# Neighbourhood stage: a third of the V loads and the gate-product stores on POOL's queue, bias tables asked for one unit sooner

## Chip, cores and metric

One core of a Trainium2 chip runs the whole kernel. The metric is device time in microseconds of one execution; the number given is the median of several runs. Engines are named as in the profile: PE (matmul), PEld (its weight loads), DVE (vector), ACT (scalar), POOL (GpSimd) and SP (which only issues transfers). "SPq" and "POOLq" are the transfers that SP and POOL issue.

## What is computed

One encoder layer on 1024 tokens (a 16 x 64 grid) with 1024 features: RMS norm, one input projection into eight parts, a dense differential attention (4 heads), a neighbourhood attention (8 heads), a gate on each, one output projection, a residual add, and a gated per-layer embedding. The part that the change touches:

```python
def neighbourhood_attention(q, k, v, rpb):
    # each query attends to its clamped 8 x 16 neighbourhood on the grid
    s = jnp.einsum('bhrcd,bhrikd->bhrcik', qg, kg) * (d ** -0.5) + bias[None]
    s = jnp.where(valid[:, None, :], s, NEG)
    pr = jax.nn.softmax(s.reshape(B, H, R, GRID_W, kr * GRID_W), axis=-1)
    o = jnp.einsum('bhrcik,bhrikd->bhrcd', pr, vg)
...
    ya = oa.transpose(0, 2, 1, 3).reshape(B, S, W_A) * jax.nn.silu(za)
    yb = neighbourhood_attention(qb, kb, vb, na_rpb[i]) * jax.nn.silu(zb)
```

## The kernel before

The program runs in stages: the input projection (to about 300 us), the neighbourhood attention (about 300 to 480), the differential attention (to about 670), and the output with the last gate. The order of the instructions on every engine is that of the Python code; there is no scheduler.

The neighbourhood stage works through 32 units: four pairs of heads (`pr`), two halves of the grid rows (`R`), four column strips (`j`). Unit 8 is the first of pair 1, unit 16 of pair 2, unit 24 of pair 3. A unit passes through these steps: `na_s` (PE: scores, line 647), `na_e` (DVE adds the bias table `Rt[pr]` and takes the minimum, line 662; ACT takes the exponential, line 667), `na_n` (DVE, lines 673 and 675), `na_t` (PE transposes, line 685; ACT copies out, line 687), `na_pv` (PE: times V, line 700) and `na_y` (DVE multiplies with the gate product into `nay`, line 710; ACT and POOL split it into a high and a low part `yb`, lines 715 and 716). After the eighth unit of a pair POOL stores both parts of `yb` to DRAM.

The stage's loop (line 1285) runs over i. Iteration i holds, in this order, `pre(i + 1)` (loads), `na_t` of unit i-1, `na_e` of unit i, `na_y` of unit i-2, `na_n` of unit i, `na_s` of unit i+1 and `na_pv` of unit i-1. Between them `fill` puts matmuls of the gate projection on PE (`z_mm`, lines 582 to 584), some ten matmuls per unit; each half of 512 tokens ends with ACT's tanh into `zth` (line 588) and DVE's product with the projection (`fin`, line 591). The product of a `zb` column stays in SBUF for `na_y`; that of a `za` column is stored to the DRAM tensor `uad` for the stage after, in two halves per column, eight stores in all.

`pre` (line 832) issues the loads: Q per half, K per pair, the two bias tables R of the next pair (`load_r`, 376 KB each), and with every unit the V window of the unit two further on (`load_v`, line 629): three transfers of 48 or 64 KB, each of four grid rows by 24 or 32 columns by 128 features. All loads go by `ld` on SP, one in-order queue; `stp` issues on POOL, another. The helper lines in the profile are 97 (`ld`), 100 (`st`) and 103 (`stp`).

SBUF tiles come from pools of rotating buffers. V windows, `nay` and `zth` share one pool of 11 buffers (tag `b2`), so a tile of the gate product frees its buffer for one of these only when its store has landed. R tables and the score tiles `nas` share one of 6.

Of the kernel before, what the change touches and what calls it, by code (L numbers as in the profile page):

```python
# [15 lines left out]
P = 128  # L16
# [8 lines left out]
COL = dict(qa=0, ka=512, va=1024, za=1536, qb=2048, kb=2560, vb=3072, zb=3584)  # L25
COL0 = (0, 8, 24, 40)
# [5 lines left out]
def ap_of(t, off, dims):  # L32
    return bass.AP(tensor=t.tensor, offset=t.offset + off, ap=[list(d) for d in dims])
# [7 lines left out]
def layer_kernel(ctx, tc, x, p, ngr, w_in, w_out, gains, lamv, t5p, rpbp, w_gate, w_ple,  # L41
# [22 lines left out]
    def T2(shape, dt=F32, n="t2"):  # L64
        return sb.tile(shape, dt, name=nm(n), tag="b2", bufs=NB2)

    def T15(shape, dt=F32, n="t15"):
        return sb.tile(shape, dt, name=nm(n), tag="b2", bufs=NB2)
# [14 lines left out]
    def PS(shape, n="ps"):  # L83
        return psp.tile(shape, F32, name=nm(n), tag="ps", bufs=4)
# [4 lines left out]
    def DT(shape, dt=F32, n="d"):  # L89
        n = nm(n)  # L90
        return dr.tile(shape, dt, name=n, tag=n, bufs=1)

    def raw(a):
        return a.bitcast(F32) if a.dtype == F32R else a

    def ld(o, i):
        return nc.sync.dma_start(raw(o), raw(i))  # L97

    def st(o, i):
        return nc.sync.dma_start(raw(o), raw(i))  # L100

    def stp(o, i):
        return nc.gpsimd.dma_start(raw(o), raw(i))
# [233 lines left out]
    def xh(kc, a, b):  # L337
        return xq(kc, a // 512)[0][:, kc % 4, a % 512:a % 512 + b - a]

    def xl(kc, a, b):  # L340
        return xq(kc, a // 512)[1][:, kc % 4, a % 512:a % 512 + b - a]
# [77 lines left out]
    vbd = DT([S, 512], n="vb")  # L419
# [147 lines left out]
    def z_low():  # L567
        while zl:
            zl.pop(0)()
# [5 lines left out]
    def z_mm(col, us):  # L575
        z_low()
        w = zw[col]
        for hf in range(2):
            a, b = hf * 512, hf * 512 + 512
            ps = PS([P, 512], "zps")  # L580
            for kc in range(8):
                mm(ps, w[:, 0, kc], xh(kc, a, b), start=(kc == 0), stop=False)  # L582
                mm(ps, w[:, 0, kc], xl(kc, a, b), start=False, stop=False)  # L583
                mm(ps, w[:, 1, kc], xh(kc, a, b), start=False, stop=(kc == 7))  # L584
                if kc < 7:
                    yield 3
            th = T2([P, 512], n="zth")
            act(th, ps, AF.Tanh, scale=0.5)

            def fin(th=th, ps=ps, hf=hf):  # L590
                V.scalar_tensor_tensor(th, th, 1.0, ps, op0=OP.add, op1=OP.mult)
                us[hf] = th
                if col < COL["qb"]:
                    st(uad[(col - COL["za"]) // P][:, hf * 512:hf * 512 + 512], th)

            zp.append(fin)
            yield 3


    uad = DT([4, P, S], n="uad")  # L600
# [6 lines left out]
    def load_k(pr):  # L607
        k1 = T8([P, 2, S], F32R, n="K1")
        h, l = qkd["kb"]
        for (dst, s) in ((k1[0:64], h), (k1[64:128], l), (K2[pr % 2][0:64], h)):  # L610
            ld(dst, s[pr].rearrange("(h d) s -> d h s", h=2))
        kb[pr] = k1

    def load_q(pr, R):
        q1 = T4([P, 2, 512], F32R, n="Q1")
        h, l = qkd["qb"]
        for (dst, s) in ((q1[0:64], h), (q1[64:128], h), (Q2[R][0:64], l)):
            ld(dst, s[pr, :, R * 512:(R + 1) * 512].rearrange("(h d) s -> d h s", h=2))
        qb[pr, R] = q1

    def load_r(pr):
        r = []
        for h in range(2):
            t = TA([P, 752], n="R")
            ld(t, ap_of(rpbp, (2 * pr + h) * 23 * 48 + 1, [[48, 8], [1, 16], [1, 752]]))
            r.append(t)
        Rt[pr] = r

    def load_v(pr, R, j):
        w = WID[j]  # L630
        v = T15([P, 3, P], n="Vw")
        for m in range(3):
            r0 = 4 * R + 4 * m
            ld(v[0:4 * w, m], ap_of(vbd, (r0 * 64 + COL0[j]) * 512 + pr * P, [[64 * 512, 4], [512, w], [1, P]]))
        Vw[pr, R, j] = v

    na = {}
# [194 lines left out]
    def pre(i):  # L832
        if i >= len(units):
            return
        pr, R, j = units[i]
        if j == 0:
            if R == 0:
                load_q(pr, 1)
            elif pr + 1 < 4:
                load_q(pr + 1, 0)  # L840
        if (R, j) == (0, 2) and pr + 1 < 4:
            load_k(pr + 1)
        if (R, j) == (1, 2) and pr + 1 < 4:
            load_r(pr + 1)
        if i + 2 < len(units):
            load_v(*units[i + 2])
# [89 lines left out]
    def s7():  # L936
# [14 lines left out]
        NS - 5: lambda: (load_r0(), x_reload()),  # L951
        NS - 4: lambda: (z_load(COL["zb"], True), z_load(COL["zb"] + P, True)),
        NS - 2: lambda: (na_consts_q(), load_q(0, 0), load_v(0, 0, 0), load_v(0, 0, 1), z_split(COL["zb"], 0, 4),
                         z_split(COL["zb"], 4, 8), z_low()),
        NS - 1: lambda: (pre(0), x_resplit()),
        NS: na_consts_k,
    }
# [327 lines left out]
    for i in range(NU + 3):  # L1285
        if i < NU:
            pre(i + 1)
# [171 lines left out]
```

## Time and profile before

| what | value |
|---|---|
| median of 3 runs | 829.63 us (827.16 to 831.23) |
| the execution profiled | 825.45 us |
| its span, first to last instruction | 823.7 us |
| PE busy | 781.7 us, 95% of the span |
| DVE, ACT, POOL busy | 514.6, 437.2 and 261.3 us |
| mean granted TensorE clock | 0.984 |
| SP's queue (q1) | 116688 packets, 145.39 MB |
| POOL's queue (q0) | 1792 packets, 5.77 MB |

The span is 1.75 us shorter than the execution. Busy time of PE counts matmuls, which are pipelined, so full stretches and holes are read from windows of time rather than from the share of the whole span. A row of the timeline gives the start and length of an instruction (or of neighbours merged into one row), its engine, its line, what it writes and reads, and in brackets the engine's idle time before it with what ended it.

### The profile page before, as it was taken

How to read it: one execution, taken by the hardware profiler on the slowest of the kernel's cores; microseconds unless marked ns; L12 is line 12 of the kernel's file. 1: busy time of each engine (PE TensorE's matmuls, PEld its weight loads, DVE VectorE, ACT ScalarE, POOL GpSimd, SP SyncE). 2: the span in 40 equal slices, each digit the busy share in tenths (PEclk: the TensorE clock that was granted, in tenths of full speed). 3: DMA queues.
4: the chain of work that ended last, by engine and by line, in shares of the span. 5: the costliest groups of instructions: out<-in, count | busy, mean ns of one | idle time of the engine just before them, and what ended most of it. 6: DMA issues, size and time to landing. Idle time of an engine off the chain costs nothing.

```text
span 823.7 us, 12188 instructions
## 1 busy us (share of the span) xinstructions
PE 781.7 (95%) x4242; PEld 647.9 (79%) x4242; DVE 514.6 (62%) x990; ACT 437.2 (53%) x814; POOL 261.3 (32%) x263
## 2 busy tenths in 40 slices
PE   7999899999989999797989988999999999999997
PEld 6788688888878887576867867888888877888886
DVE  4658976786997675445536568777777743732332
ACT  5765545254444545335635578888888852311120
POOL 1001433352655400011101035777777752100000
PEclk9999999999999999999989999999999999999999
DMA  8855363862889997585767578667577427122222
GB/s 318 321 199 185 120 212 101 283 156 85 237 262 239 239 307 198 142 232 164 213 174 194 168 219 231 169 173 209 162 211 192 161 96 281 77 89 91 93 87 90
DMA packets 118541, 151.94 MB, mean 184 GB/s; under 512 B 23848, under 2 KB 76744, under 8 KB 118352
## 3 DMA queue, kind: packets, MB, share of 16 engines
q1 hardware_dynamic: 116688, 145.39, 58.9%
q0 software_dynamic: 1792, 5.77, 2.1%
q8 instruction: 34, 0.56, 0.3%
q14 instruction: 27, 0.22, 0.1%
HBM read 104.96 MB, written 46.17 MB: 183 GB/s over the span
## 4 chain that ended last, share of the span: by engine, by line
PE 65%; DMA 11%; DVE 11%; ACT 5%; issue 3%; SPq 3%; POOL 2%; DVEq 0%; ACTq 0%; POOLq 0%
PE dsp L1066 6%; PE ips L234 6%; PE ips L236 6%; PE ips L235 6%; PE gps L1261 4%; PE gps L1259 4%; PE gps L1260 4%; DMA Vw<-vb 3%; PE dtp L1108 3%; SPq L97 2%; PE ntp L685 2%; DMA wraw<-in_w_in_dram 2%; PE dpv L1135 2%; PE zps L582 2%; PE zps L584 2%
## 5 line engine op out<-in xcount | busy, mean ns | idle before, releaser
L234 PE MATMUL ips<-w,xh 128*128 128x512 f32 x336 | 134.0, 399 | 3.6 <-DVE C L260 3.0
L236 PE MATMUL ips<-w,xl 128*128 128x512 f32 x336 | 131.8, 392 | 0.0
L235 PE MATMUL ips<-w,xh 128*128 128x512 f32 x336 | 131.3, 391 | 0.0
L1091 POOL TENSOR_TENSOR s<-s,s 128x1024 f32<-128x1024 f32 x32 | 77.1, 2408 | 57.0 <-ACT s L1090 55.3
L433 POOL TENSOR_TENSOR qrs<-qms,nhalf 128x16 f32<-128x16 f32 x16 | 51.4, 3214 | 91.1 <-DVE qms L431 91.1
L1076 DVE CUSTOM_DVE_ANT_0 s<-dsp,T 128x1024 f32<-128x1024 f32 x64 | 77.7, 1215 | 2.5 <-PE dsp L1066 2.5
L234 PEld LDWEIGHTS ips<-w,xh 128*128 128x128 f32 x336 | 63.4, 189 | 17.1 <-issue 3.8
L1078 ACT ACTIVATE s<-s,dm 128x1024 f32<-128x1024 f32 x64 | 73.3, 1146 | 4.6 <-DVE dm L1076 4.5
L1066 PE MATMUL dsp<-K,Q 128*128 128x512 f32 x256 | 69.7, 394 | 4.9 <-DVE dm L1076 4.3
L236 PEld LDWEIGHTS ips<-w,xl 128*128 128x128 f32 x336 | 63.4, 189 | 13.8
L1115 DVE TENSOR_TENSOR aTl<-dtp,aTh 128x512 fp32r<-128x512 f32 x64 | 44.2, 691 | 48.0 <-ACT aTh L1109 48.0
L235 PEld LDWEIGHTS ips<-w,xh 128*128 128x128 f32 x336 | 63.6, 189 | 12.7
L716 POOL TENSOR_TENSOR yb<-nay,yb 128x128 fp32r<-128x128 f32 x32 | 16.4, 514 | 168.8 <-ACT yb L715 168.8
L218 DVE TENSOR_TENSOR w<-wraw,w 128x512 fp32r<-128x512 f32 x84 | 62.2, 778 | 5.6 <-ACT w L217 5.5
L687 ACT ACTIVATE PT<-ntp 96x768 f32<-96x768 f32 (+1 forms) x32 | 25.9, 810 | 63.0 <-PE ntp L685 63.0
L1066 PEld LDWEIGHTS dsp<-K,Q 128*128 128x128 f32 x256 | 45.9, 189 | 14.6 <-issue 3.1
L582 PE MATMUL zps<-xh,zw 128*128 128x512 f32 x128 | 54.2, 423 | 0.0
L584 PE MATMUL zps<-xh,zw 128*128 128x512 f32 x128 | 51.3, 401 | 0.0
L583 PE MATMUL zps<-xl,zw 128*128 128x512 f32 x128 | 51.1, 399 | 0.0
L217 ACT ACTIVATE w<-wraw 128x512 fp32r<-128x512 f32 x84 | 48.4, 626 | 4.7 <-DVE wraw L193 4.7
L1109 ACT ACTIVATE aTh<-dtp 128x512 fp32r<-128x512 f32 x64 | 38.0, 593 | 23.8 <-PE dtp L1108 23.7
L1259 PE MATMUL gps<-wgh,x1h 128*128 128x512 f32 x128 | 50.5, 395 | 0.0
(177 smaller groups left out, 1820.9 us busy)
## 6 DMA issues: line engine op xcount, KB each, us to landing
wraw<-in_w_in_dram SPq DMA_DIRECT2D x72, 256.0 KB
x<-in_x_dram SPq DMA_DIRECT2D x8, 512.0 KB
ppd<-pp SPq DMA_DIRECT2D x8, 512.0 KB
K<-kbh SPq DMA_DIRECT2D x8, 512.0 KB
Q<-qbh SPq DMA_DIRECT2D x16, 256.0 KB
Q<-qah SPq DMA_DIRECT2D x16, 256.0 KB
Q<-qal SPq DMA_DIRECT2D x16, 256.0 KB
wor<-in_w_out_dram SPq DMA_DIRECT2D x8, 512.0 KB
```

Source lines behind the costliest of these rows:

```text
L218: V.tensor_tensor(w[:, 1], r, w.bitcast(F32)[:, 0], op=OP.subtract)
L234: mm(ps, lh[:, k, a:a + P], w[:, 0], start=(new and k == 0), stop=False, skip_group_check=cont)
L235: mm(ps, lh[:, k, a:a + P], w[:, 1], start=False, stop=False, skip_group_check=cont)
L236: mm(ps, ll[:, k, a:a + P], w[:, 0], start=False, stop=(k == 3), skip_group_check=cont)
L433: G.tensor_tensor(rs, ms, nhalf, op=OP.pow)
L582: mm(ps, w[:, 0, kc], xh(kc, a, b), start=(kc == 0), stop=False)
L584: mm(ps, w[:, 1, kc], xh(kc, a, b), start=False, stop=(kc == 7))
L1066: mm(ps[:, cs], q[g][:, m, u * P:(u + 1) * P], k[:, cs], start=(g == 0), stop=(g == 1))
L1076: V.tensor_tensor_reduce(out=s, in0=ps, in1=back(Td[h][:, :], 1919 - (896 - P * qt), [[-1, S]]), scale=-1.0, scalar=BIG, op0=OP.add, op1=O ...
L1078: act(s, s, AF.Exp, bias=mx, scale=-1.0, accum_out=z[:, m:m + 1])
L1091: G.tensor_tensor(s1, s1, s2, op=OP.add)
L1259: mm(ps, h[:, k], wh, start=(k == 0), stop=False)
```

## The change

Three edits. The store of a `za` gate product goes by `stp` instead of `st`, so POOL issues it. Of the three transfers of a V window the third goes by `stp`, so POOL issues that too; the first two stay on SP. The bias tables of the next pair are asked for with unit (1, 1) instead of (1, 2), which is one unit sooner in the loop.

```diff
@@ z_mm, fin
                 if col < COL["qb"]:
-                    st(uad[(col - COL["za"]) // P][:, hf * 512:hf * 512 + 512], th)
+                    stp(uad[(col - COL["za"]) // P][:, hf * 512:hf * 512 + 512], th)
@@ load_v
         for m in range(3):
             r0 = 4 * R + 4 * m
-            ld(v[0:4 * w, m], ap_of(vbd, (r0 * 64 + COL0[j]) * 512 + pr * P, [[64 * 512, 4], [512, w], [1, P]]))
+            (ld if m < 2 else stp)(v[0:4 * w, m], ap_of(vbd, (r0 * 64 + COL0[j]) * 512 + pr * P, [[64 * 512, 4], [512, w], [1, P]]))
@@ pre
-        if (R, j) == (1, 2) and pr + 1 < 4:
+        if (R, j) == (1, 1) and pr + 1 < 4:
             load_r(pr + 1)
```

On SP, at the first load of bias tables (for pair 1). `Vw` is a V window, `R` a bias table, `vb` and `in_rpb_dram` are their sources; the number tells tiles apart, x3 counts transfers:

```order
-L97 DMA Vw_2989<-vb_111 128x1x128 x3
-L97 DMA Vw_3041<-vb_111 96x1x128 x3
-L97 DMA R_3095<-in_rpb_dram 128x1x752
-L97 DMA R_3097<-in_rpb_dram 128x1x752
-L97 DMA Vw_3099<-vb_111 96x1x128 x3
-L97 DMA Vw_3151<-vb_111 128x1x128 x3
+L97 DMA Vw_2989<-vb_111 128x1x128 x2
+L97 DMA R_3041<-in_rpb_dram 128x1x752
+L97 DMA R_3043<-in_rpb_dram 128x1x752
+L97 DMA Vw_3045<-vb_111 96x1x128 x2
+L97 DMA Vw_3099<-vb_111 96x1x128 x2
+L97 DMA Vw_3151<-vb_111 128x1x128 x2
```

The tables stand one V window earlier, and every window has two transfers on SP instead of three. (A new tile name gets a new number, so Vw_3045 is the Vw_3041 of before.)

On POOL, around the first store of a gate product (at the end of pair 0; rows without a sign stood there before):

```order
+L103 DMA Vw_3316<-vb_111 96x1x128
+L103 DMA uad_115<-zth_3342 128x512
 L716 TENSOR_TENSOR yb_2963<-nay_3348,yb_2963 128x8x16
 L103 DMA ybh_116<-yb_2963 128x1024
 L103 DMA ybl_117<-yb_2963 128x1024
+L103 DMA Vw_3378<-vb_111 128x1x128
 L716 TENSOR_TENSOR yb_3403<-nay_3401,yb_3403 128x8x16
+L103 DMA Vw_3433<-vb_111 128x1x128
```

The third of a V window now stands ahead of each subtraction, and the store between a V third and a subtraction. The same place on SP loses the store:

```order
-L97 DMA Vw_3316<-vb_111 96x1x128 x3
-L100 DMA uad_115<-zth_3342 128x512
-L97 DMA Vw_3378<-vb_111 128x1x128 x3
+L97 DMA Vw_3316<-vb_111 96x1x128 x2
+L97 DMA Vw_3378<-vb_111 128x1x128 x2
```

On SP nothing waits for the gate product any more; the next V window follows the one before it.

## Rows read from the trace of the kernel before

**Rows 1.** Stretches: busy us (instructions) of PE, PEld, DVE, ACT, POOL; clock; DMA share; GB/s.

```profile
300.00:340.00 40.00, 37.97 (x243) 30.17 (x242) 24.84 (x75) 21.04 (x54) 2.98 (x6) 1.00 0.76 200
340.00:450.00 110.00, 96.01 (x636) 75.90 (x636) 52.84 (x174) 50.33 (x132) 13.53 (x25) 0.94 0.66 188
450.00:480.00 30.00, 30.00 (x199) 23.87 (x199) 15.96 (x46) 16.53 (x42) 3.07 (x7) 1.00 0.51 138
```

**Rows 2.** Timeline of PE, 340 to 430 us: start, length, engine, line, [idle before it].

```profile
348.69 1.65 PE L647 MATMUL nsp<-K,Q 128*128 128x384 f32 x4 [4.35 <-DVE nam L662]
...
373.14 0.88 PE L700 MATMUL npv<-PT,Vw 96*64 96x128 f32 x12 [1.50 <-ACT PT L687]
375.16 0.83 PE L685 MATMUL ntp<-idn,nas 128*96 128x128 f32 x6 [1.14 <-DVE nas L675]
...
385.64 1.02 PE L685 MATMUL ntp<-idn,nas 128*128 128x128 f32 x6 [1.84 <-DVE nas L675]
...
422.26 1.51 PE L685 MATMUL ntp<-idn,nas 128*128 128x128 f32 x6 [4.08 <-DVE nas L675]
```

**Rows 3.** Stretches behind the two long holes, same columns as rows 1.

```profile
348.70:353.25 4.55, 4.55 (x20) 3.47 (x21) 2.20 (x8) 0.80 (x3) 0.46 (x1) 0.50 0.83 192
422.30:428.40 6.10, 6.10 (x19) 4.88 (x19) 3.50 (x13) 2.20 (x6) 0.62 (x2) 0.50 0.74 226
```

**Rows 4.** Waits, 295 to 480 us: engine and line <- awaited: total us, times, longest.

```profile
DVE nas L662 <- DMA R<-in_rpb_dram: 7.6, 2, 6.0
...
ACT zth L588 <- DMA uad<-zth: 5.7, 1, 5.7
...
DVE nay L710 <- DMA uad<-zth: 5.1, 2, 4.1
```

**Rows 5.** Timeline of SP's queue: start and length of the issue.

```profile
339.58 1.29 SPq L97 DMA_DIRECT2D R<-in_rpb_dram  x2
...
363.84 1.22 SPq L100 DMA_DIRECT2D uad<-zth  x1
...
380.60 1.39 SPq L97 DMA_DIRECT2D R<-in_rpb_dram  x2
...
414.74 1.73 SPq L100 DMA_DIRECT2D uad<-zth  x1
...
418.90 1.35 SPq L97 DMA_DIRECT2D R<-in_rpb_dram  x2
```

**Rows 6.** Chain of work that ended last: start, length, what (transposes of unit 4).

```profile
326.66 0.79 PE ntp L685 x6
```

**Rows 7.** Timelines of DVE and ACT (the row L588).

```profile
348.17 0.46 DVE L662 CUSTOM_DVE_ANT_1 nas<-nsp,R 128x288 f32<-128x288 f32 x1 [1.51 <-DMA R<-in_rpb_dram]
...
356.60 0.69 DVE L591 SCALAR_TENSOR_TENSOR zth<-zth,zps 128x512 f32<-128x512 f32 x1 [5.17 <-ACT zth L588]
...
371.80 0.60 ACT L588 ACTIVATE zth<-zps 128x512 f32<-128x512 f32 x1 [5.74 <-DMA uad<-zth]
...
389.94 0.45 DVE L662 CUSTOM_DVE_ANT_1 nas<-nsp,R 128x288 f32<-128x288 f32 x1
...
405.49 0.68 DVE L591 SCALAR_TENSOR_TENSOR zth<-zth,zps 128x512 f32<-128x512 f32 x1
...
421.30 0.29 DVE L710 TENSOR_TENSOR nay<-npv,zth 128x128 f32<-128x128 f32 x1 [4.11 <-DMA uad<-zth]
...
433.13 0.45 DVE L662 CUSTOM_DVE_ANT_1 nas<-nsp,R 128x288 f32<-128x288 f32 x1
```

**Rows 8.** POOL: issues of line 103 (ns min/median/max), their landing, and subtractions (busy, mean ns).

```profile
L103 POOL DMA_DIRECT2D ybh<-yb x4: 571/580/721, 358.3 to 480.1; - x4
...
DMA to landing us min/median/max: 4.3/7.0/10.4
...
L716 POOL TENSOR_TENSOR yb<-nay,yb 128x128 fp32r<-128x128 f32 x32 | 16.4, 514 | 168.8 <-ACT yb L715 168.8
```

**Rows 9.** Stretch around the first R issue, same columns as rows 1.

```profile
338.00:341.00 3.00, 2.03 (x10) 1.64 (x10) 1.11 (x3) 1.18 (x5) 0.46 (x1) 1.00 0.32 84
```

## Prediction

> **What bounds the kernel now.** I read the sums by stretch first. In the neighbourhood stage (about 300 to 480 us) PE, the matmul engine, is the busiest: 30.00 of 30 us in the last stretch, 37.97 of 40 in the first, but 96.01 of 110 in the middle, with a granted clock of 0.94 there and 1.00 on either side [rows 1]. So the stage is bound by PE, except for 14.0 us of holes and a slower clock between 340 and 450. Next PE in order of time: five holes make 12.9 of these 14.0 us, 4.35 before unit 9's scores at 348.69, 1.50 and 1.14 near 374, 1.84 at 385.64 and 4.08 at 422.26 [rows 2]. [...]
>
> Then the waits, for who made the holes. DVE waited 7.6 us for the bias tables R, ACT 5.7 us once and DVE 5.1 us twice for stores of the gate product to `uad` [rows 4]. Both are transfers of SP's queue. SP reaches the first R load at 339.58 [rows 5], though the loop asks for it in iteration 5, whose first PE work, `na_t` of unit 4, starts at 326.66 [rows 6]: the queue runs 13 us behind the program. R is used at once when it lands, the second head at 348.17 [rows 7], 8.6 us after the issue. The stores are the same story: DVE ends the product at 357.29 (356.60 + 0.69), SP issues its store at 363.84, and ACT, whose next `zth` takes the stored tile's buffer, has idled 5.74 us when it goes on at 371.80; the third product ends at 406.17 (405.49 + 0.68), its store goes out at 414.74, and DVE's `nay` waits 4.11 us for it, to 421.30 [rows 5, 7]. The hole of 1.84 us is the second store, the remaining 1.0 of DVE's 5.1 us [rows 2, 4]. So three late stores and one late table make all five holes.
>
> **The change, part by part.**
>
> 1. *R one unit sooner.* R is put ahead of one unit's V loads, and of the seven units' loads ahead of it one third each is gone: ten issues fewer on SP before it (three for the unit passed, seven thirds). From one R pair to the next SP took 41.0 us (339.58 to 380.60 [rows 5]) for 39 issues (2 R, 24 V, 6 Q, 3 K, 2 gate weights, 2 stores), 1.05 us each. At that price R leaves SP 10.5 us sooner, at 329; at the price of an issue alone (1.29 us for the two R [rows 5], 0.65 each) 6.5 us sooner, at 333. PE lost 4.35 us by R, so either covers it: 4.35 + 2.28 = **6.6 us** gone.
>
> 2. *Stores from POOL's queue.* A store on POOL stands behind a V third and in front of a `yb` subtraction, and waits for the same DVE product. Nothing of SP's backlog stands ahead of it. POOL's own 512 KB stores land 4.3 to 10.4 us after issue, 7.0 in the median, and an issue takes 0.57 to 0.72 us of POOL [rows 8]. From the end of the product to the need there are 8.8 us for the first (357.29 to 366.06, where ACT's idle time began) and 11.0 us for the third (406.17 to 417.19) [rows 7]. The stores have half those bytes. So they are in time except at the slow end: 1.50 + 1.14 + 1.84 + 4.08 of holes and 3.05 of half clock, **11.6 us**.
>
> 3. *A third of the V loads from POOL.* 32 issues leave SP and come to POOL. No V load from POOL's queue is in this trace; the nearest rows are the 512 KB stores, 0.57 to 0.72 us an issue [rows 8]. POOL now has 0.51 us of work per unit [rows 8], and a unit takes 4.5 us (43.2 us from unit 16's first R use to unit 24's, less 7.1 us of hole and half clock, over eight [rows 7]). With 0.72 for the load it is 1.2 of 4.5: hidden beside PE. Without that cover it would be 32 x 0.72 = 23 us at the most, so the cover matters, and it is wide: 3.3 us a unit. The load is asked for about four units before `na_pv` reads it, 18 us against 10.4 at most for landing. What is queued behind it on POOL is a `yb` subtraction, whose reader is the store at the end of eight units. In the stage after, one store stands between POOL's additions, some 0.7 us once beside PE work.
>
> Sum: 18.2 us gone. What is late next? Between 340 and 450 the other 1.1 us of holes stay. The first stretch had 2.03 us of small holes in 40 us without any of these waits, the last none in 30 [rows 1]; at the first's rate 110 us would hold 5.6, so 4.5 may come back, at the last's none. The stretch resembles the first more (K, Q and R are still loaded), so I give back 2.5. Net 15.7 us: 825.45 - 15.7 = 809.8 for the execution profiled. That one lies 4.18 us under the median of the runs; the median becomes 829.63 - 15.7 = **813.9**, given as 814.
>
> A row that bears on steps 1 and 3: from 338 to 341 us, just around R's issue, the DMA engines moved 84 GB/s at a mean busy share of 0.32 [rows 9]. The six transfers directly ahead of R are V thirds, so a V third seems to keep few engines busy while the queue behind it stands. [...]
>
> **The rivals.**
>
> *The DMA engines stay the limit (chance 0.20).* If a V third from POOL occupies the same engines as one from SP, the seven thirds save R nothing; it gains only its place, three issues, 3.2 us, and the queue's pace stays. For: the share of 0.32 above, a few engines working while the rest wait. Then PE can't get far ahead of the tables. With 8.6 us from issue, the third pair (418.90 [rows 5]) is usable at 427.5 against a use at 433.13 [rows 7], 5.6 us of room, and 3.2 more for its place: PE comes forward 8.8 us at most until there, the rest is waited again. Time 829.63 - 8.8 = 820.8. [...]
>
> *The stores stay late (0.13).* POOL takes its list in order, and the V third ahead of the store waits for a buffer that PE or POOL itself frees. If that holds the store back as long as SP did (6.55 us for the first), the 11.6 us stay and only R's 6.6 go, less the 2.5: 825.5, on the edge of no change. Against: the buffer's last reader is an iteration old by then.
>
> *POOL becomes the bound: slower (0.07).* If an issue of 128 short rows takes POOL far longer than of 128 long ones, POOL's list per unit, 0.51 us and one issue, outgrows a unit's 4.5 us; `nay` buffers come free late and `na_y` and the V loads wait for them. It decides from 4.0 us an issue on, and at 4.6 it has eaten the gain (28 units at 0.56). At 5.0 us: 28.0 - 15.7 = 12.3 us slower, 842. Against: 0.57 to 0.72 in the nearest rows.
>
> That the change doesn't do what it says is excluded by the order of instructions: POOL has 40 transfers more, SP 32 V thirds and 8 stores fewer.
>
> **How the numbers follow.** Forecast 0.60, engines 0.20, late stores 0.13, POOL 0.07. Half a per cent, 4.1 us, is about what a measurement of this kernel can tell from no change. The first two are faster by more than that, the third within it: faster 0.80, same 0.13, slower 0.07. The low end has all 18.2 us, the 1.1 and the first stretch's 2.03 gone, from the profiled execution's own time: 825.45 - 21.3 = 804. The high end takes in the late stores: 826.
>
> **What would show it.** Right: no DVE wait for R above 1 us, no wait for `uad` on ACT or DVE, the clock at 1.00 through 340 to 450 and PE's idle time there under 6 us; R issued before 333 us; POOL's V issues under 1 us. Engines as the limit: waits for R at units 16 and 24 and R pairs still some 40 us apart. Late stores: `uad` waits of 4 us again, with POOL idle in front of a V load. POOL as the bound: POOL's issues of several us and DVE waiting for POOL. The prediction fails if PE's holes move instead of going, above all to `na_pv` waiting for a third of V.

## The result, and the profile after

The changed kernel takes 821.68 us in the median (819.55 to 823.30) against 829.63 before (five executions of each): a ratio of 0.9904, 95% interval 0.9874 to 0.9934. It is 7.95 us faster. The forecast was 814.0, 15.6 us faster: right in sign, inside the range (804 to 826, which took in nearly no change), twice too large in size. The execution profiled took 819.77 us, with a span of 818.0.

The sums by stretch of the changed kernel, columns as in [rows 1]:

```profile
300.00:340.00 40.00, 38.09 (x243) 30.13 (x242) 23.89 (x73) 20.05 (x49) 6.21 (x10) 1.00 0.87 222
340.00:450.00 110.00, 102.20 (x688) 80.66 (x687) 56.84 (x188) 55.81 (x150) 32.60 (x53) 0.97 0.76 187
450.00:480.00 30.00, 28.59 (x180) 22.63 (x177) 18.83 (x45) 17.65 (x36) 6.67 (x11) 1.00 0.95 267
```

PE's idle time between 340 and 450 us fell from 14.0 to 7.8 us and the clock rose from 0.94 to 0.97: better, but not the stage without long holes that the forecast had. What fills the 7.8 us is in the waits of 290 to 480 us (engine and line, what was awaited, total us, times, longest), against [rows 4]:

```profile
PE npv L700 <- DMA Vw<-vb: 5.1, 4, 1.9
PEld npv L700 <- DMA Vw<-vb: 4.2, 3, 2.1
...
DVE nas L662 <- DMA R<-in_rpb_dram: 2.8, 3, 1.7
```

Both `uad` waits are gone and the wait for R fell from 7.6 to 2.8 us. In their place PE waits for V windows, which it did nowhere in [rows 2]. PE's holes over 0.8 us in this stretch, from its timeline as in [rows 2]:

```profile
346.16 0.98 PE L647 MATMUL nsp<-K,Q 128*128 128x384 f32 x4 [1.36 <-DVE nam L662]
372.69 0.44 PE L700 MATMUL npv<-PT,Vw 96*64 96x128 f32 x4 [0.91 <-DMA Vw<-vb]
374.61 0.95 PE L700 MATMUL npv<-PT,Vw 96*64 96x128 f32 x8 [1.48 <-DMA Vw<-vb]
413.77 0.44 PE L700 MATMUL npv<-PT,Vw 96*64 96x128 f32 x4 [0.84 <-DMA Vw<-vb]
416.07 1.12 PE L700 MATMUL npv<-PT,Vw 96*64 96x128 f32 x8 [1.86 <-DMA Vw<-vb]
```

Behind each pair of `npv` holes the granted clock is at half for 3.42 us (columns as in [rows 3]):

```profile
374.83:378.25 3.42, 3.42 (x18) 2.80 (x15) 0.00 (x0) 1.12 (x2) 0.00 (x0) 0.50 0.44 119
415.79:419.21 3.42, 3.14 (x16) 2.71 (x17) 0.29 (x1) 0.45 (x1) 0.00 (x0) 0.50 0.71 198
```

So 18.2 us of holes and half clock went, and 1.36 + 5.09 + 3.42 (half of twice 3.42) = 9.9 us came back: 8.3 us by this count, 7.95 by the medians (the two executions profiled are 5.7 us apart). The thirds that PE waited for were SP's: taking the last update of a transfer's semaphore in the trace as its landing, SP's thirds landed at 372.55, 374.56, 413.64 and 416.03, each at most 0.14 us before PE went on, and the first and third of them had been issued 13.9 us earlier; POOL's thirds of the same two windows had landed at 354.97 and 396.80. The question for the runs is why these V windows became late as soon as R and the stores were early.

The SP issues that the prediction followed, against [rows 5]: R leaves before 333 us, as forecast, but the next pairs follow 41.7 and 41.5 us apart, and behind the three K loads SP takes 8.43 us for four V issues (start, length of the issues, tile, count).

```profile
332.92 1.88 SPq L97 DMA_DIRECT2D R<-in_rpb_dram  x2
...
354.85 0.62 SPq L97 DMA_DIRECT2D K<-kbh  x1
355.51 1.06 SPq L97 DMA_DIRECT2D K<-kbl  x1
356.61 1.94 SPq L97 DMA_DIRECT2D K<-kbh  x1
358.66 8.43 SPq L97 DMA_DIRECT2D Vw<-vb  x4
...
374.58 1.31 SPq L97 DMA_DIRECT2D R<-in_rpb_dram  x2
...
416.04 1.70 SPq L97 DMA_DIRECT2D R<-in_rpb_dram  x2
```

POOL's groups after (busy us, mean ns; idle before): a V issue takes 694 ns there, next to the 0.72 that the prediction took from [rows 8], and the stores wait for DVE alone.

```profile
L103 POOL DMA_DIRECT2D Vw<-vb x29 | 20.1, 694 | 1.7 <-issue 0.7 <-POOL yb L716 0.4 <-PE zps L584 0.2
...
L103 POOL DMA_DIRECT2D uad<-zth x7 | 4.0, 576 | 20.8 <-DVE nay L710 12.6 <-DVE narz L673 8.3
```

### The profile page after: what moved, and what is told of

Read it like the earlier page. It is cut to its first block, busy times and chain, and to the rows that moved or that the text cites. A ratio compares the mean times of both kernels' runs of the same rounds, so it can differ in the third digit from the quotient of the medians.

```text
span 818.0 us, 12241 instructions
## 1 busy us (share of the span) xinstructions
PE 782.3 (96%) x4242; PEld 647.7 (79%) x4242; DVE 514.4 (63%) x990; ACT 437.4 (53%) x814; POOL 289.1 (35%) x303
## 4 chain that ended last, share of the span: by engine, by line
PE 67%; DMA 10%; DVE 9%; ACT 4%; SPq 4%; issue 3%; POOL 1%; DVEq 0%; POOLq 0%; ACTq 0%
PE ips L234 6%; PE ips L236 6%; PE ips L235 6%; PE dsp L1066 6%; DMA Vw<-vb 5%; PE gps L1259 4%; PE gps L1261 4%; PE gps L1260 4%; SPq L97 4%; PE dtp L1108 3%; PE ntp L685 2%; PE pps L314 2%; PE dpv L1135 2%; PE oap L1230 2%; PE npv L700 2%
## 5 line engine op out<-in xcount | busy, mean ns | idle before, releaser
L236 PEld LDWEIGHTS ips<-w,xl 128*128 128x128 f32 x336 | 63.8, 190 | 13.9
L235 PEld LDWEIGHTS ips<-w,xh 128*128 128x128 f32 x336 | 63.9, 190 | 12.7
L716 POOL TENSOR_TENSOR yb<-nay,yb 128x128 fp32r<-128x128 f32 x32 | 18.1, 564 | 113.0 <-ACT yb L715 105.6
L1263 ACT ACTIVATE gth<-gps 128x512 f32<-128x512 f32 x16 | 9.6, 597 | 77.2 <-PE gps L1261 72.4
```

The lines of the kernel that those rows point to most:

```text
L235: mm(ps, lh[:, k, a:a + P], w[:, 1], start=False, stop=False, skip_group_check=cont)
L236: mm(ps, ll[:, k, a:a + P], w[:, 0], start=False, stop=(k == 3), skip_group_check=cont)
```

## Experiments

Each of twelve kernels was timed against the kernel before on the same chip (827.87 us for e1 to e4; 828.28, 828.27 and 828.07 for the later ones). Ratios are to that, with 95% intervals; a gain or cost in us below is worked out from the ratios, on 828 us.

| run | what it is | us | ratio | waits for R / `uad` / V, us |
|---|---|---|---|---|
| e1_stores | stores alone | 825.53 | 0.9969 (0.9955 to 0.9983) | 17.9 / 0 / 0.9 |
| e2_tables | tables sooner alone | 834.24 | 1.0091 (1.0059 to 1.0122) | 5.4 / 18.8 / 0.4 |
| e3_v_third | V third alone | 823.85 | 0.9962 (0.9945 to 0.9978) | 5.7 / 10.0 / 0.4 |
| e4_stores_tables | stores and tables | 829.26 | 1.0025 (1.0008 to 1.0042) | 14.6 / 0 / 11.6 |
| f2_stores_v | stores and V third | 820.03 | 0.9895 (0.9869 to 0.9921) | 13.1 / 0 / 0 |
| the change | all three | 821.68 | 0.9904 (0.9874 to 0.9934) | 2.8 / 0 / 9.3 |
| e5_k_spread | the change, K in three parts | 824.79 | 0.9965 (0.9947 to 0.9983) | 14.6 / 0 / 4.6 |
| f1_v_pool | stores, all V from POOL | 820.43 | 0.9898 (0.9868 to 0.9928) | 0 / 1.7 / 0.4 |
| f3_v_cols | outer dimension of half the V loads | 817.13 | 0.9868 (0.9843 to 0.9894) | 1.7 / 9.3 / 0 |
| g1_cols_stores | f3 and stores | 811.71 | 0.9801 (0.9776 to 0.9826) | 4.9 / 0 / 0 |
| g2_change_cols | f3 and the change | 816.28 | 0.9835 (0.9806 to 0.9864) | 4.4 / 0 / 0.7 |
| g3_cols_stores_v32 | g1, V thirds of wide strips from POOL | 812.69 | 0.9800 (0.9773 to 0.9826) | 4.2 / 0 / 0.4 |
| h1_cols_stores_tables | g1 and tables sooner | 815.23 | 0.9840 (0.9812 to 0.9868) | 12.0 / 0 / 0.4 |

The last column sums the waits of DVE for R, of ACT and DVE for `uad`, and of PE and its weight loads at `npv` for V, all from 290 to 480 us of the profiled execution; the second half of a V wait overlaps the first.

### The parts one by one

Each takes one or two of the change's three edits; the diffs here and below are shortened where `...` stands.

```diff
 e1_stores, e4_stores_tables, f2_stores_v
-                    st(uad[...], th)
+                    stp(uad[...], th)
 e3_v_third, f2_stores_v
-            ld(v[0:4 * w, m], ...)
+            (ld if m < 2 else stp)(v[0:4 * w, m], ...)
 e2_tables, e4_stores_tables
-        if (R, j) == (1, 2) and pr + 1 < 4:
+        if (R, j) == (1, 1) and pr + 1 < 4:
```

> The kernel before with the first edit alone: the gate-product stores on POOL's queue. Theory A (V behind K): what limits the changed kernel is that SP's own V windows, queued behind the three 512 KB loads of K, land late; PE's holes at na_pv for V (0.91 + 1.48 + 0.84 + 1.86 = 5.1 us, and two half-clock stretches of 3.41 us, half of each lost) ate the gain. Then a PE that is held by R for 4.35 us at unit 9 loses less at na_pv, and the stores alone give nearly all: 821 to 823 us, no wait for uad left. Theory B (the parts add): the stores give 11.6 us less what comes back, and R's hole stays whole, 827 us (821.7 of the changed kernel plus 6.6 for R less the 1.36 of R still seen there).

> The second edit alone: bias tables one unit sooner. Theory A: the hole of 4.35 us at unit 9 shrinks, but the stores leave SP when the queue gets to them, at the same time as before, so PE waits the rest there: 827 to 830 us, uad waits on ACT and DVE of 5 us or more each. Theory B: R's 6.6 us less 1.36 us are gained whatever else waits: 824 us.

> The third edit alone: a third of every V window from POOL's queue, stores and tables as before. Theory A: the number of issues does not set SP's pace (R pairs were 41.7 and 41.5 us apart in the changed kernel with 29 issues, 41.0 and 38.3 before with 39), so R and the stores are as late as before: 827 to 831 us. Theory B: seven to ten issues fewer ahead of R and of each store bring these 7 us forward, enough for all of the waits for them: 818 to 823 us.

> The change without the third edit: stores from POOL, tables one unit sooner, all V from SP. Theory A: as the changed kernel within 2 us, 820 to 824, with the same waits of PE for V. Theory B: the V windows come from the longer queue, PE's waits for V grow from 9.3 to 15 us or more, and the time goes to 826 or more.

> The change without its second edit: stores and a third of V from POOL, tables at their old place. If putting R a unit sooner only costs (6.4 us alone, 3.7 beside the stores), because 752 KB then stand in front of V windows and the K loads that are needed as soon: 816 to 818 us. If the tables' place pays once the queue is relieved, R's hole at unit 9 comes back: 824 us or more, with DVE waiting 4 us or more for R.

Measured: 825.53, 834.24, 823.85, 829.26 and 820.03 us. Theory A falls with e3 and e4. Theory B holds there, nearly; in e1 the time lies between the two theories, 1.5 us under B's, and in e2 it lies outside both. f2 lies between its two cases. The stores alone give 2.6 us where 11.6 us of holes went. In e1_stores the holes stand elsewhere, at the first use of R in every pair (PE's timeline):

```profile
348.71 1.65 PE L647 MATMUL nsp<-K,Q 128*128 128x384 f32 x4 [5.30 <-DVE nam L662]
...
390.31 0.98 PE L647 MATMUL nsp<-K,Q 128*128 128x384 f32 x4 [1.91 <-DVE nam L662]
...
433.77 1.65 PE L647 MATMUL nsp<-K,Q 128*128 128x384 f32 x4 [5.48 <-DVE nam L662]
```

The tables a unit sooner alone *cost* 7.5 us, more than either theory allowed. The hole at unit 8 shrinks, then ACT waits 12.23 us for one `uad` store and PE stands for 7.92. ACT's timeline in e2_tables:

```profile
374.74 0.60 ACT L588 ACTIVATE zth<-zps 128x512 f32<-128x512 f32 x1 [12.23 <-DMA uad<-zth]
```

and PE's, behind it:

```profile
376.08 1.55 PE L700 MATMUL npv<-PT,Vw 96*64 96x128 f32 x12 [7.92 <-ACT PT L687]
```

A third of V from POOL gives 3.1 us alone, and stores and third together 8.7, the whole gain of the change: each is worth about twice as much beside the other, and the second edit adds nothing to them (0.9895 and 0.9904, the intervals overlap), though without it DVE waits 13.1 us for R. Read down the table, the three waits trade places. Before, they were 7.6, 10.8 and 0.3 us, 18.7 together; in e1, e2 and e4, which leave all of V on SP, they sum to 18.8, 24.6 and 26.2, and with a third of V from POOL to 16.1 in e3 and 13.1 in f2. What the first three brought forward made something else late by as much or more. That points to the queue's rate rather than its order; the next runs try this.

### Is it the K loads in front of V?

```diff
 e5_k_spread, against the changed kernel
-        if (R, j) == (0, 2) and pr + 1 < 4:
-            load_k(pr + 1)
+        if R == 0 and j >= 1 and pr + 1 < 4:
+            load_k_part(pr + 1, j - 1)
```

`load_k_part` issues one of the three loads that `load_k` issues.

> The changed kernel with the three K loads of the next pair asked for one each with units (0, 1), (0, 2) and (0, 3) instead of all three with (0, 2). Theory A (V behind K): the V windows of SP no longer stand behind 1.5 MB, PE's waits for V (9.3 us) and the half-clock stretches behind them go: 813 to 816 us. Theory E (few engines): the bytes ahead of the later V windows and of R are the same, the waits move to other units: 819 to 822 us.

Measured 824.79 us. PE's waits for V at `npv` halved (9.3 to 4.6), and those for R grew from 2.8 to 14.6: the waits moved to other units, and the time was a little worse than theory E's range. Theory A falls. K in front of V decides where the queue is felt, not whether.

### How many DMA engines a V window uses

All V from POOL takes 24 transfers per pair of heads off SP; the other run leaves every transfer on SP, with the same bytes and pieces, and changes only its outer dimension.

```diff
 f1_v_pool, with the stores from POOL
-            ld(v[0:4 * w, m], ...)
+            stp(v[0:4 * w, m], ...)
 f3_v_cols
+            if w == 24:
+                ld(v[0:96, m], ap_of(vbd, (4 * R * 64 + COL0[j] + m) * 512 + pr * P, [[64 * 512, 12], [3 * 512, 8], [1, P]]))
+            else:
                 ld(v[0:4 * w, m], ap_of(vbd, ..., [[64 * 512, 4], [512, w], [1, P]]))
...
-   nc.tensor.transpose(tp[...], s[:, h, m * k4:(m + 1) * k4], idn)
+   nc.tensor.transpose(tp[...], (s[:, h, m:m + 3 * k4 - 2:3] if WID[j] == 24 else s[:, h, m * k4:(m + 1) * k4]), idn)
```

> The stores and all three thirds of every V window from POOL's queue, tables at their old place. Theory E (few engines): a V third from SP keeps only some four of the 16 DMA engines busy (83 to 90 GB/s at a share of 0.2 to 0.3 in the stretches in which V moves alone), 0.6 to 0.8 us each, 24 of them 17 us of the 41 us from one R pair to the next, and what follows on SP waits behind them; from POOL they leave these engines. With none left on SP the queue runs ahead of PE: no wait for R, for uad or for V above 1 us, and all of the 18.2 us come: 811 to 814 us. Rival P (POOL's order): POOL takes its list in order, and three issues of 0.7 us per unit stand behind a subtraction that waits for ACT; V then lands late from POOL, PE waits for it at na_pv, 820 us or more.

> The kernel before, with the V windows of the strips of 24 columns loaded in another order: third m holds every third column of all 12 rows instead of all columns of 4 rows, and the transposes read the scores in the same order. The number of transfers, their bytes and the size of their pieces (512 bytes) stay, and all stay on SP; only the outer dimension of the transfer is 12 instead of 4. Theory E: if the outer dimension sets how many DMA engines share a transfer, half of the thirds take 0.2 us instead of 0.6 on the engines that hold the queue, 12 x 0.4 = 5 us per pair of heads, about what taking a third of V away does: 823 to 826 us. Rival N (number of transfers): SP has at most eight transfers in flight, each some 7 us from issue to landing, so only the number of transfers counts: 827 to 829 us, no change.

f3_v_cols takes 817.13 us: 10.9 us faster than the kernel before without taking one transfer off SP, where the rival had no change. Theory E had 823 to 826; the direction is its own, the size well beyond it. The same 10 us of both kernels show it, 334 to 344 us in 40 slices of 0.25 us: mean busy share of the DMA engines in tenths, and GB/s. First the kernel before, with R's first issue at 339.58 [rows 5]:

```profile
DMA  9899999975232222222222232236484545444445
GB/s 188 158 258 258 236 201 281 213 148 98 74 129 88 102 72 84 80 78 92 82 86 84 84 66 70 82 86 116 98 90 156 191 141 141 129 126 96 120 120 144
```

and f3_v_cols:

```profile
DMA  6632255224555345555746454658654746356532
GB/s 143 145 62 61 88 156 150 82 82 137 154 110 97 113 149 153 133 111 107 113 101 143 116 156 144 210 219 262 144 156 108 186 180 156 112 172 135 133 116 80
```

Before, the engines run at two tenths and some 80 GB/s for most of 4 us, while R waits in line; with twelve rows outermost this plateau is gone, and R is issued at 335.60. The semaphore records show it for single transfers. A V third of four rows on SP's queue gets one update just after its issue and 4 as it lands (all 96 of the kernel before), in f3_v_cols one of twelve rows gets 1 and 12, and Q and K get 16. Before, the six thirds ahead of R landed 0.55 to 0.81 us apart (339.95, 340.74, 341.55, 342.17, 342.82, 343.37); in f3_v_cols the three of twelve rows ahead of R landed 0.2 us apart (339.39, 339.60, 339.79). The plateau at a share of 0.2 to 0.3 (the work of three to five of 16 engines, an estimate from the share alone), its end, and the 4 and 12 updates agree with four rows being spread over fewer DMA engines than twelve. No view here names the engines, so the few engines stay an inference; shown are the outer dimension, the share and the spacing. The edit also changes the order in which the transposes read the scores; their mean length is 284 ns there and 286 before, and that of their weight loads 154 and 136, so PE's own work did not get shorter.

f1_v_pool takes 820.43 us, well above theory E's 811 to 814. The time is in rival P's range, but its reason is not seen: PE's weight loads wait 0.4 us for V in all. The execution profiled is its fastest (815.45); what the slower ones lost beyond it is not shown. From 340 to 450 us it does what E said, PE at 106.92 of 110 us and the clock at 1.00. It loses time at the stage's start, as its stretches show against [rows 1]:

```profile
300.00:340.00 40.00, 34.12 (x205) 27.46 (x204) 20.40 (x63) 16.56 (x41) 12.22 (x19) 0.91 1.03 234
340.00:450.00 110.00, 106.92 (x745) 85.18 (x745) 62.02 (x205) 60.83 (x161) 63.77 (x102) 1.00 0.98 204
```

In PE's timeline the loss is a hole of 4.54 us for Q:

```profile
308.87 0.58 PE L647 MATMUL nsp<-K,Q 128*128 128x288 f32 x1 [4.54 <-DMA Q<-qbh]
```

With all of V from POOL the DMA engines are busy throughout (1.03 and 0.98), and SP's transfers land late: the first Q, issued at 294.10, landed at 306.85, 12.8 us later, where before it took 8.1 (293.15 to 301.27), and R took 13.3 to 18.9 us in place of 6.2 to 8.1. Transfers from POOL's queue slow SP's here.

### What stays when the queue is relieved

```diff
 g1_cols_stores: f3_v_cols with
-                    st(uad[...], th)
+                    stp(uad[...], th)
 g2_change_cols: the changed kernel with f3's two edits
 g3_cols_stores_v32: g1_cols_stores with (32-column strips alone)
-                ld(v[0:4 * w, m], ...)
+                (ld if m < 2 else stp)(v[0:4 * w, m], ...)
 h1_cols_stores_tables: g1_cols_stores with
-        if (R, j) == (1, 2) and pr + 1 < 4:
+        if (R, j) == (1, 1) and pr + 1 < 4:
```

> The V windows of the 24-column strips with the outer dimension of 12, and the first edit of the change (stores from POOL); no third from POOL, tables at their old place. Theory E (few engines): the run with the columns alone still had PE's holes of 1.24, 1.14, 1.24 and 3.30 us behind late stores and 3.41 us of half clock; without them 817.1 - 6.9 - 1.7 = 808.5 us, range 806 to 812. Rival Q (SP's queue is only just relieved): with the stores gone PE runs up against the tables again, as it did in the run with the stores alone: holes of 3 us or more at units 8, 16 or 24 with DVE waiting for R, 814 us or more.

> The changed kernel, all three edits, with the outer dimension of 12 in the V windows of the 24-column strips, on either queue. Theory E: what was given back in the changed kernel was SP's V thirds, late because their four engines hold the queue; PE's holes at na_pv (5.1 us) and their half clock (3.4 us of time) go: 821.7 - 8.5 = 813 us or less, 807 to 813. Theory A (V behind K): V still stands behind 1.5 MB of K, so the waits at na_pv stay at 5 us or more and the time at 818 to 822.

> As the run with columns and stores, and one third of the V windows of the 32-column strips from POOL: of the 12 transfers per pair that still use few engines four more leave SP. Theory E: no slower, 0 to 3 us faster than that run, 805 to 811 us. Rival P (POOL's transfers cost the others): as in the run with all V from POOL, SP's own transfers land later (the first Q, 4.5 us), and it is 2 us or more slower than that run.

> The run with columns and stores (811.7 us) and the second edit of the change, tables one unit sooner. Alone and beside the stores this edit cost 6.4 and 3.7 us. If it costs because the tables then stand ahead of V windows on a queue that is late already, it costs nothing on a relieved queue and gains at most the hole of 1.85 us that this run still had at unit 8: 809.8 to 812.5 us. If it costs by itself (the tables' 752 KB collide with something at their new place), 815 to 818 us; that would also account for the 4.6 us by which the changed kernel with the columns was slower than this run.

g1_cols_stores takes 811.71 us (811.45 to 813.90), the best of all: 2.0% faster than the kernel before, and its interval ends below the change's. It lies in E's range, at its upper end. The stores, worth 2.6 us alone, are worth 5.5 here, with no other wait taking their place but one of 1.85 us at unit 8. PE's stretch:

```profile
340.00:450.00 110.00, 105.56 (x731) 83.34 (x730) 62.99 (x203) 58.74 (x155) 17.94 (x34) 1.00 0.78 206
```

g2_change_cols takes 816.28 (812.66 in the execution profiled), 3.3 us above theory E's 813; but its waits at `npv` for V fall from 9.3 to 0.7 us, which theory A excluded. So the V waits of the change hung on the outer dimension of V's transfers, as theory E has it. g3 is the same as g1 within the intervals, 812.69 us, just above theory E's 805 to 811 and without rival P's 2 us: with the columns, thirds from POOL bring nothing.

h1_cols_stores_tables bears on the second edit: 815.23 us, the time that "costs by itself" had. DVE's waits for R *grow* when R is asked for sooner. The table's own view, issue lengths in ns (min/median/max, first and last start in us) and who waited. In g1_cols_stores:

```profile
L97 SPq DMA_DIRECT2D R<-in_rpb_dram x6: 613/631/855, 336.8 to 411.3; - x6
...
  DVE nas L665: 4.9, 3
```

and in h1_cols_stores_tables:

```profile
L97 SPq DMA_DIRECT2D R<-in_rpb_dram x6: 622/1414/2058, 331.8 to 415.9; - x6
...
  DVE nas L665: 12.0, 6
```

The unit passed is a 24-column strip. At its old place R stands behind that strip's V, at the new one directly behind the V of a 32-column strip, still on four rows; its issue takes 1.41 us in place of 0.63 and its landing 11.2 us from the issue in place of 7.6 (medians), and it is late in every pair. That this place is the reason fits the rows, but no run changes it alone.

## Why the prediction was half right

**Reading of the bound.** Right: PE with holes from SP's late transfers. The reason for the lateness was not pursued far enough. Row 9 (84 GB/s at 0.32 [rows 9]) was in the prediction as a remark on steps 1 and 3; f3_v_cols, 10.9 us faster with the outer dimension of half of these transfers raised from 4 to 12, shows that it was the larger part of the bound.

**Step 1, R a unit sooner, 6.6 us.** Half of it happened as written: R left SP at 332.92 us, at the 333 worked out from the price of an issue alone, and PE's hole shrank from 4.35 to 1.36 us. The other half failed: "either covers it" took 8.6 us from issue to use for granted, and now the second head's table is used at 345.64, 12.7 us after the issue, and still waited for:

```profile
345.64 0.46 DVE L662 CUSTOM_DVE_ANT_1 nas<-nsp,R 128x288 f32<-128x288 f32 x1 [1.66 <-DMA R<-in_rpb_dram]
```

That is DVE's timeline of the changed kernel, against 348.17 in [rows 7]: leaving 6.7 us sooner brought R 2.5 us. And the edit is worth nothing: with the stores and the V third, the kernel is as fast without it (820.03 against 821.68); in the three other pairs of runs it costs 7.5 (alone), 4.6 (beside the stores) and 3.2 us (beside stores and columns, where the intervals overlap a little).

**Step 2, the stores, 11.6 us.** All `uad` waits went, as forecast, and POOL issues the stores in 576 ns. The term was mis-sized: alone they gave 2.6 us. Holes of 5.30, 1.91 and 5.48 us for R took their place, since PE, freed from one late transfer, ran up to the next of the same queue. The half clock in this step and the first, 3.05 and 2.28 us, is half of the 6.10 and 4.55 us at a clock of 0.50 in [rows 3]; PE's timeline before has the gate matmuls starting 0.43 us apart there (350.14, 350.56, 350.99) and 0.23 us apart at 1.00 (354.06, 354.29, 354.52), so the half is nearly what these lost.

**Step 3, a V third from POOL.** "Hidden" was right, at 694 ns an issue. Its use was counted only in R's earlier issue of step 1; it gave 3.1 us alone and 6.1 beside the stores (the stores 2.6 alone and 5.5 beside it), so the gain belongs to the two together, and the 6.6 us of step 1 stand in the sum for an edit that gave none.

**The sum.** Here the prediction went wrong: "4.5 may come back ... I give back 2.5" measured 9.9 us. The holes were added as if independent, and the give-back was read from small holes of a neighbouring stretch. They were one queue's lateness, seen at five places; the rivals' "PE can't get far ahead of the tables", which gave 820.8, used the right picture, though its mechanism (the POOL third on SP's engines, saving nothing) is against e3_v_third, 3.1 us faster. Which engines a third uses no view shows; in the changed kernel's trace each of POOL's 32 V thirds has 16 semaphore updates and each of SP's 64 has 1 and 4, so the two don't look alike. Of the signs listed, R before 333 us, no `uad` waits and POOL's issues under 1 us came; the clock (0.97 for 1.00), PE's idle time (7.8 for under 6) and the longest wait for R (1.7 for 1) missed, and the sign named as failure, holes that move to `na_pv` waiting for V, came. Two signs of the first rival came as well: R pairs still some 40 us apart (41.7 and 41.5), and waits for R at units 16 and 24, small ones (0.20 and 0.95 us). That the time fell inside the range owes something to luck: a term of 6.6 us too much, one of 11.6 that was 2.6 alone, and a third edit put at nothing that gave 3.1 to 6.1 partly cancelled.

**What stays open.** Why the R edit did so much harm in e2_tables was not tried by itself. The traces suggest a collision. In 0.5 us slices from 352 to 372 us, tenths of DMA share and GB/s, the kernel before:

```profile
DMA  9983469983222239998999999999999894222379
GB/s 211 238 156 81 131 170 321 317 193 95 83 86 87 85 117 264 208 300 354 418 401 410 434 385 410 401 377 279 205 238 221 197 304 121 83 84 92 110 229 302
```

and e2_tables:

```profile
DMA  9893469999999932589999999989979622772222
GB/s 212 190 246 61 149 152 286 329 355 340 419 388 396 359 121 112 139 208 359 266 186 152 218 229 164 216 165 231 254 164 238 115 82 74 274 275 79 66 67 84
```

Before, POOL's two `yb` stores (issued at 358.30 and 358.88) and SP's three K loads (from 358.21) moved together, and the core carried 354 to 434 GB/s from 361 to 365.5 us. In e2_tables PE is earlier and the stores go out at 354.77, over V windows; K is no earlier, and from 361.5 to 367.5 the core carries 152 to 266. The `uad` store behind K is what ACT waits 12.23 us for. Its semaphore records say where it was held: 12 of its 16 updates came from 370.11 to 370.48 us, the other four only from 373.52 to 374.65, and ACT went on at 374.74; the same store before had its last four at 371.03 to 371.44. Four updates that lag are as many as a V third of four rows gets as it lands, which would fit V thirds in front on the same few engines; no view names the engines, so this is my guess. That the collision costs the 7.5 us is argued, not shown.

## What to carry to other kernels

When several engines wait for different transfers of one in-order queue, don't add the holes: ask what rate the queue has and what in it moves at a low DMA share, because taking away one wait may only bring PE to the next (in e1_stores the waits for `uad` went from 10.8 us to 0 and those for R from 7.6 to 17.9). Look at the DMA share in the stretch just ahead of a late transfer; a plateau of two or three tenths there can mean, as here, that the transfers in front have a small outer dimension, and a larger one may be worth more than moving transfers to another queue or asking sooner (10.9 us here, against 8.7 for stores and V third and a cost of 7.5 for the tables). Test each edit of a bundle by itself: here two gave 2.6 and 3.1 us alone and 8.7 together, and one was dead weight or worse.

## What the runs showed of the hardware that I had not expected

The outer dimension of half of the V transfers, 4 to 12 at the same bytes, count and queue, was worth 1.3% of the kernel (0.9868, 0.9843 to 0.9894). A transfer from POOL beside one from SP seems to raise the rate of the core, 354 to 434 GB/s with stores and K together against 152 to 266 with K after the stores; this is one pair of traces and no test; with the engines busy throughout (a share of 1.03 in f1_v_pool) the first Q on SP's queue took 12.8 us to land in place of 8.1. And a transfer asked for sooner was awaited longer: 12.0 us in h1_cols_stores_tables in place of 4.9 in g1_cols_stores.
